# RMSNorm's weight before two gemms and its 1/rms behind them, in one decoder layer on one core

## The chip, the cores and the metric

One NeuronCore of a Trainium2 chip runs the whole program. The metric is device microseconds of one execution; the time of a kernel is the median of its runs. PE is TensorE, DVE is VectorE, ACT is ScalarE, POOL is GpSimd, and SP (SyncE) issues the DMAs. A line number such as L900 is a line of the kernel before; in the kernel after, lines behind the edits have other numbers.

## The reference

One layer, 512 positions (SEQ), width 1024 (D_MODEL), feed-forward width 4096, all fp32. The first half, retention and windowed attention merged by gates, is not touched by the change. Its second half is:

```python
def rmsnorm(x, g):
    y = x * rsqrt(mean(x * x, axis=-1) + EPS)
    return y * g
...
x = x + merged @ w_o
x = x + square(relu(rmsnorm(x, g_mlp) @ w_up)) @ w_down
x = x + sigmoid(rmsnorm(x, g_ple) @ w_ple_gate) * (p_i @ w_ple_proj)
```

For a row of x, 1/rms is one number r. Since relu(r a)^2 = r^2 relu(a)^2, and a gemm is linear in each row, r may be applied at the output: as r^2 where the MLP's product is added to x, as r inside the sigmoid.

## The kernel before

**Numbers and tiles.** x lies in four row tiles `xs[t]` of 128 x 1024 (t = 0 to 3). Every fp32 operand of a gemm is split in a high and a low half, and each product is three matmuls (`mm3`, L256 to L258): high x high, high x low, low x high. For the weights, ACT makes the high half (`whi`, L223) and the DVE the low one (`wlo`, L224), from a raw tile of 128 x 1024 that SP loads. There are six raw buffers and four of each half. The weights follow one plan; `units(n)` takes the next n tiles and first prepares `AHEAD` = 2 more. Some tiles of the down projection are sums or differences of two loads, which the DVE makes first (L202, L205).

**Order.** The kernel is plain Python that emits the instructions; a scheduler then orders each engine's queue and hands out the buffers. Work that should stand between matmuls is put into a list with `later(lag, ...)`. `tick()`, called from inside the gemms, emits what has become due; `force(key)` emits everything up to the entry named.

**The tail** (`tail`) is the stage of the change:

1. The W_o gemm, in two halves of 512 output columns, added into `xs` by the DVE. The second half's consumer `last` also starts `norm_T` of the tile, which gives h2.
2. `norm_T` (L381 on): two Squares on ACT with a sum per row (L388), the mean on the DVE (L390, L354), the power -1/2 on POOL (L355), two tensor_scalar y = x r (L394), and per half of 512 columns a `split_T`: four transposes on PE into one PSUM bank (`pt`, L365), four copies on ACT with the weight's column as scale (L373) and four scalar_tensor_tensor of 128 x 128 on the DVE for the low half (L374).
3. Four FFN phases f = 0 to 3. Each has an up gemm over 1024 of the 4096 features (192 matmuls of 512 columns), relu and square, sums of quarters of the result (`seven_left`), and the down projection `seven_gemm`: seven products in place of eight. Its units run in the order 4, 3, 5 (first unit), 4, 3, 5 (second unit), then 2, 2, 1, 1, 7, 7, 6, 6; a unit is 12 matmuls. The finished products are added to or subtracted from the 512-column quarters of x by the DVE (`acc`, L900), right behind the product that ends them.
4. In the last phase `ready` runs `norm_T` on each tile for h3: tiles 0 and 1 behind product 7, tiles 2 and 3 behind product 6.
5. The gate gemm (`w_ple_gate`) in two halves, sigmoid on ACT (L1001), times the embedding product, plus x (L1002, L1003), and out. Before a tile's matmuls `need` forces h3 of that tile.

Of the kernel before, what the change touches and what calls it, by code (L numbers as in the profile page):

```python
# [11 lines left out]
F32 = mybir.dt.float32  # L12
F32R = mybir.dt.float32r
AF = mybir.ActivationFunctionType
ALU = mybir.AluOpType
AX = mybir.AxisListType

P = 128
S = 512
D = 1024  # L20
NT = S // P
KD = D // P
# [6 lines left out]
EPS = 1e-6  # L29
# [3 lines left out]
GG = (2, 4)  # L33
# [42 lines left out]
class Block:  # L76
# [183 lines left out]
    def rows_gemm(self, act, nk, consume, perm=False, group=2, need=None, wave=None, halves=False):  # L260

        banks = [None] * NT
        nu = nk // 2
        if wave is not None:
            us = []

            def part(t, u):
                if u == 0:
                    banks[t] = self.gbank()
                wh, wl = us[u]  # L270
                for k in range(2):
                    kk = 2 * u + k
                    sh, sl = self.stat(act, kk, t, perm)
                    self.mm3(banks[t], sh, sl, wh[:, k], wl[:, k], kk == 0, kk == nk - 1)
                if u == nu - 1:
                    consume(t, banks[t])

            for m in range(NT):
                self.pinned = True
                if m >= 2:  # L280
                    wave(m)
                us += self.units(1)
                if m < NT - 1:
                    for t in range(m):
                        part(t, m)
                self.force(("h", m, 1))
                if m < NT - 1:
                    for u in range(m + 1):
                        part(m, u)
                self.pinned = False  # L290
            for t in range(NT - 1):
                part(t, NT - 1)
                part(NT - 1, t)
                self.ahead(t + 1)
            part(NT - 1, NT - 1)
            return
        for u0 in range(0, nu, group):
            us = self.units(min(group, nu - u0))
            for t in range(NT):
                if need is not None:  # L300
                    need(t)
                if u0 == 0:
                    banks[t] = self.gbank()
                cols = [slice(0, 512)] if not (halves and t == NT - 1) else [slice(0, 256), slice(256, 512)]
                for c in cols:
                    if c.start:
                        banks[t] = self.gbank()
                    for u, (wh, wl) in enumerate(us):
                        for k in range(2):
                            kk = 2 * (u0 + u) + k  # L310
                            sh, sl = self.stat(act, kk, t, perm)
                            self.mm3(banks[t][:, c], sh, sl, wh[:, k, c], wl[:, k, c], kk == 0, kk == nk - 1)
                        if u0 + u < nu - 1:
                            self.tick()
                    if u0 + len(us) == nu:
                        if len(cols) > 1:
                            consume(t, banks[t], c)
                        else:
                            consume(t, banks[t])
                        self.tick()  # L320
# [61 lines left out]
    def norm_T(self, x, t, goff, dst, key, lag):  # L382

        nc = self.nc
        ss = self.small(2, "ss")
        for h in range(2):
            j = self.tmp("j")
            self.pin(nc.scalar.activation(j, x[:, h * 512 : (h + 1) * 512], AF.Square, accum_out=ss[:, h : h + 1]))  # L388
        s1 = self.small(1, "s1")
        nc.vector.tensor_tensor(s1, ss[:, 0:1], ss[:, 1:2], op=ALU.add)  # L390
        r = self.rstd(s1, 1, D)
        for h in range(2):
            y = self.tmp("y")
            nc.vector.tensor_scalar(y, x[:, h * 512 : (h + 1) * 512], r, None, op0=ALU.mult)  # L394
            gain = None if goff is None else lambda k: self.gcol[:, goff + k : goff + k + 1]
            self.later(lag, lambda y=y, h=h: self.split_T([y], t, gain, 4 * h, dst), (key, t, h))

    def new_act(self, nbig, s):
        return ([self.big(s + "h") for _ in range(nbig)], [self.big(s + "l") for _ in range(nbig)])
# [474 lines left out]
        nc.scalar.activation(R(hi), src, AF.Copy)  # L874
        nc.vector.tensor_tensor(R(lo), src, hi, op=ALU.subtract)

    def seven_gemm(self, U, xs, ready):


        nc = self.nc  # L880
        LEFT = {1: 3, 2: 4, 3: 0, 4: 6, 5: 1, 6: 5, 7: 2}
        banks = {}

        def product(m, bank, u, first, last):
            (wh, wl), = self.units(1)
            for p in range(2):
                if first:
                    banks[bank, p] = self.gbank() if m in (3, 4) else self.bank("pb")
                ps = banks[bank, p]
                for k in range(2):  # L890
                    kk = 2 * u + k
                    c = slice(LEFT[m] * 256 + p * P, LEFT[m] * 256 + (p + 1) * P)
                    sh, sl = (R(U[i][kk].rearrange("p a b -> p (a b)")[:, c]) for i in range(2))
                    self.mm3(ps, sh, sl, wh[:, k], wl[:, k], first and k == 0, last and k == 1, m != bank)
                self.tick()

        X = lambda i, j, p: xs[2 * i + p][:, 512 * j : 512 * (j + 1)]

        def acc(x, v, op=ALU.add):
            nc.vector.tensor_tensor(x, x, v, op=op)  # L900

        for u in range(2):
            for m in (4, 3, 5):
                product(m, m, u, u == 0, u == 1)
        m4 = []
        for p in range(2):
            t = self.tmp("m4")
            nc.scalar.activation(t, banks[4, p], AF.Copy)
            m4.append(t)
            acc(X(0, 1, p), banks[3, p])  # L910
            acc(X(0, 1, p), banks[5, p], ALU.subtract)
        for u in range(2):
            product(2, 4, u, False, u == 1)
        for p in range(2):
            acc(X(1, 0, p), banks[4, p])
            acc(X(1, 1, p), banks[4, p], ALU.subtract)
        for u in range(2):
            product(1, 1, u, u == 0, u == 1)
        for p in range(2):
            acc(m4[p], banks[1, p])  # L920
            acc(X(0, 0, p), m4[p])
            acc(X(1, 1, p), m4[p])
        for u in range(2):
            product(7, 5, u, False, u == 1)
        for p in range(2):
            acc(X(0, 0, p), banks[5, p])
            if ready is not None:
                ready(p)
        for u in range(2):
            product(6, 3, u, False, u == 1)  # L930
        for p in range(2):
            acc(X(1, 1, p), banks[3, p])
            if ready is not None:
                ready(2 + p)


    def tail(self, mx):
        nc, a = self.nc, self.a
        xb = [self.big("x1") for _ in range(2)]
        xs = [xb[t // 2].rearrange("p (t c) n -> p t (c n)", t=2)[:, t % 2] for t in range(NT)]  # L940
# [3 lines left out]
        def add(half):  # L944
            def f(t, ps):
                v = xs[t][:, half * 512 : (half + 1) * 512]
                nc.vector.tensor_tensor(v, v, ps, op=ALU.add)
            return f

        self.rows_gemm(mx, KD, add(0))  # L950
        h2 = self.new_act(2, "h2")

        def last(t, ps):
            add(1)(t, ps)
            self.norm_T(xs[t], t, 16, h2, "h2", 5)

        self.rows_gemm(mx, KD, last, group=4)

        h3 = None
        for f in range(NF // 2):  # L960
            U = [[self.big("uh") for _ in range(4)], [self.big("ul") for _ in range(4)]]
# [28 lines left out]
            ready = None  # L990
            if f == NF // 2 - 1:
                h3 = self.new_act(2, "h3")
                ready = lambda t: self.norm_T(xs[t], t, 24, h3, "h3", 2 if t < 2 else 0)
            self.seven_gemm(U, xs, ready)

        out = self.a["out"][0]
        for half in range(2):
            def fin(t, ps, i=slice(0, 512)):
                s, o = self.tmp("fs"), self.tmp("fo")
                c = slice(half * 512 + i.start, half * 512 + i.stop)  # L1000
                nc.scalar.activation(s[:, i], ps[:, i], AF.Sigmoid)  # L1001
                nc.vector.tensor_tensor(o[:, i], s[:, i], pp[half][:, t, i], op=ALU.mult)  # L1002
                nc.vector.tensor_tensor(s[:, i], o[:, i], xs[t][:, c], op=ALU.add)  # L1003
                nc.sync.dma_start(out[t * P : (t + 1) * P, c], s[:, i])

            self.rows_gemm(h3, KD, fin, need=lambda t: self.force(("h3", t, 1)), group=GG[half], halves=half == 1)

    def make_plan(self):
        a, w = self.a, self.w_in
# [53 lines left out]
```

## Time and profile before

| | |
|---|---|
| median of 3 runs | 1037.51 us (1036.36 to 1038.64) |
| the profiled execution | 1038.66 us, span 1036.7 us |
| mean granted TensorE clock | 0.996 |
| the tail in the span, roughly | 640 to 1036.7 us |
| down projection of phase 0 ends | 738 us |
| down projection of phase 3 ends, gate gemm starts | 984.6 us |

The span goes from the first to the last instruction; the profiled execution is 1.96 us longer than it, which lies around it. A row of a timeline has start, duration, engine, line, operation, output <- inputs, shape and xcount, and in brackets an idle time before it and what ended it. A row of grouped instructions has the count, then busy time, then the mean in ns of one, then the idle time before them. A duration reaches past the start of the next instruction on the same engine, so that equal instructions in a row start closer together than they last.

### The profile page before, as it was taken

To read this page: it belongs to the slowest core of one execution; us is meant where nothing else is said; L and a number is where in the kernel's file an instruction comes from. 1 tells how busy PE (TensorE), PEld (TensorE's weight loads), DVE (VectorE), ACT (ScalarE), POOL (GpSimd) and SP (SyncE) were. 2 spreads that over 40 slices of the span, in tenths; PEclk is the share of its full clock that TensorE was granted. 3 is DMA by queue.
4 is the path that set the end of the run, shared out by engine and by line. 5 is a ranking of instruction groups with operands and counts; after the bars stand their busy time and mean duration, and the time that the engine had idled before them with its cause. 6 is when DMAs were issued, how large, how long until landed. Compare 5 with 4: busy or idle time off the path is not lost.

```text
span 1036.7 us, 12913 instructions
## 1 busy us (share of the span) xinstructions
PE 1014.2 (98%) x4810; PEld 848.4 (82%) x4810; DVE 676.6 (65%) x1017; ACT 480.4 (46%) x1012; POOL 137.8 (13%) x126
## 2 busy tenths in 40 slices
PE   8998989999999999999999999999999999999998
PEld 6776878988987788888888888988888888888877
DVE  5588766767686743545343344679769877867983
ACT  6534635465452442535342323665455355355461
POOL 0264043123025501000010000000000000000000
PEclk9999999999999999999999999999999999999999
DMA  9532312323321222222323422354753753845711
GB/s 330 180 116 69 99 42 63 101 62 102 102 69 54 82 82 81 82 82 68 96 89 115 162 85 78 103 183 161 233 175 124 241 166 120 265 160 184 243 63 59
DMA packets 84766, 128.81 MB, mean 124 GB/s; under 512 B 6576, under 2 KB 39392, under 8 KB 84704
## 3 DMA queue, kind: packets, MB, share of 16 engines
q1 hardware_dynamic: 84704, 128.00, 38.7%
q8 instruction: 37, 0.61, 0.2%
q14 instruction: 25, 0.20, 0.1%
HBM read 123.77 MB, written 4.21 MB: 123 GB/s over the span
## 4 chain that ended last, share of the span: by engine, by line
PE 81%; DVE 8%; issue 2%; POOL 2%; ACT 1%; DMA 0%; DVEq 0%; ACTq 0%; POOLq 0%
PE pg L256 23%; PE pg L258 23%; PE pg L257 23%; DVE ro L510 2%; PE pb L256 2%; PE pb L258 2%; PE pb L257 2%; DVE wlo L224 1%; PE ph L522 1%; DVE wlo L229 1%; PE pt L365 1%; POOL r L355 1%; PE po L638 1%; PE sc L615 1%; DVE ro L512 1%
## 5 line engine op out<-in xcount | busy, mean ns | idle before, releaser
L256 PE MATMUL pg<-whi,hh 128*128 128x512 f32 x480 | 201.7, 421 | 1.6 <-ACT zn L552 0.8
L257 PE MATMUL pg<-wlo,hh 128*128 128x512 f32 x480 | 189.7, 395 | 2.1 <-DVE wlo L229 2.1
L258 PE MATMUL pg<-whi,hl 128*128 128x512 f32 x480 | 189.5, 395 | 0.0
L223 ACT ACTIVATE whi<-raw 128x1024 fp32r<-128x1024 f32 (+1 forms) x120 | 123.6, 1043 | 131.9 <-PE pg L257 39.0
L224 DVE TENSOR_TENSOR wlo<-raw,whi 128x1024 fp32r<-128x1024 f32 (+1 forms) x120 | 146.2, 1230 | 36.8 <-ACT whi L223 35.7
L229 DVE SCALAR_TENSOR_TENSOR wlo<-raw,gcol,whi 128x512 fp32r<-128x512 f32 (+1 forms) x184 | 122.2, 704 | 64.1 <-ACT whi L228 63.9
L228 ACT ACTIVATE whi<-raw,gcol 128x512 fp32r<-128x512 f32 (+1 forms) x184 | 107.4, 639 | 86.3 <-PE pg L258 53.1
L355 POOL TENSOR_TENSOR r<-v,mhalf 128x1 f32<-128x1 f32 (+1 forms) x52 | 40.5, 778 | 653.0 <-DVE v L354 653.0
L257 PEld LDWEIGHTS pg<-wlo,hh 128*128 128x128 f32 x480 | 99.3, 207 | 18.2 <-DVE wlo L229 4.6
L258 PEld LDWEIGHTS pg<-whi,hl 128*128 128x128 f32 x480 | 98.6, 205 | 17.4 <-DVE hl L379 0.4
L256 PEld LDWEIGHTS pg<-whi,hh 128*128 128x128 f32 x480 | 98.9, 206 | 16.2 <-ACT whi L228 1.2
L256 PE MATMUL pg<-h2h,whi 128*128 128x512 f32 (+1 forms) x288 | 105.5, 367 | 0.0
L257 PE MATMUL pg<-h2l,whi 128*128 128x512 f32 (+1 forms) x288 | 105.3, 366 | 0.0
L258 PE MATMUL pg<-h2h,wlo 128*128 128x512 f32 (+1 forms) x288 | 105.2, 366 | 0.0
L258 PEld LDWEIGHTS pg<-h2h,wlo 128*128 128x128 f32 x288 | 54.3, 189 | 8.8
L257 PEld LDWEIGHTS pg<-h2l,whi 128*128 128x128 f32 x288 | 54.3, 189 | 8.6
L256 PEld LDWEIGHTS pg<-h2h,whi 128*128 128x128 f32 x288 | 54.2, 189 | 8.7
L256 PE MATMUL pg<-hh,whi 128*128 128x512 f32 x128 | 52.4, 410 | 0.0
L257 PE MATMUL pg<-wlo,uh 128*128 128x512 f32 x128 | 50.1, 391 | 0.0
L258 PE MATMUL pg<-hh,wlo 128*128 128x512 f32 x128 | 50.0, 391 | 0.0
L257 PE MATMUL pg<-hl,whi 128*128 128x512 f32 x128 | 49.9, 390 | 0.0
L258 PE MATMUL pg<-whi,ul 128*128 128x512 f32 x128 | 49.9, 390 | 0.0
(176 smaller groups left out, 1838.4 us busy)
## 6 DMA issues: line engine op xcount, KB each, us to landing
raw<-in_w_down SPq DMA_DIRECT2D x80, 512.0 KB, 3.4
raw<-in_w_in SPq DMA_DIRECT2D x76, 512.0 KB, 3.8
raw<-in_w_up SPq DMA_DIRECT2D x32, 512.0 KB, 4.6
raw<-in_w_ret_out SPq DMA_DIRECT2D x8, 512.0 KB, 3.4
raw<-in_w_o SPq DMA_DIRECT2D x8, 512.0 KB, 3.5
raw<-in_w_ple_gate SPq DMA_DIRECT2D x8, 512.0 KB, 4.8
x<-in_x SPq DMA_DIRECT2D x8, 256.0 KB, 6.1
pp_dram<-pp SPq DMA_DIRECT2D x8, 256.0 KB, 4.1
```

The source lines that it names most:

```text
L223: self.pin(nc.scalar.activation(R(hi[:, i]), raw[:, i], AF.Copy))
L224: nc.vector.tensor_tensor(R(lo[:, i]), raw[:, i], hi[:, i], op=ALU.subtract)
L228: self.pin(nc.scalar.activation(R(hi[:, i]), raw[:, i], AF.Copy, scale=g))
L229: nc.vector.scalar_tensor_tensor(R(lo[:, i]), raw[:, i], g, hi[:, i], op0=ALU.mult, op1=ALU.subtract)
L256: t.matmul(ps, sh, mh, start=first, stop=False, skip_group_check=more)
L257: t.matmul(ps, sh, ml, start=False, stop=False, skip_group_check=more)
L258: t.matmul(ps, sl, mh, start=False, stop=last, skip_group_check=more)
L355: self.nc.gpsimd.tensor_tensor(r, v, self.mhalf[:, :w], op=ALU.pow)
L365: nc.tensor.transpose(ps[:, k * P : (k + 1) * P], part[:, k * P : (k + 1) * P], self.ident)
L510: nc.vector.tensor_tensor(v4(t2)[:, :, o0 : o0 + 64], v4(zn)[:, :, i0 : i0 + 64], bc(Sn[:, o0 : o0 + 64], 64), op=ALU.mult)
L512: nc.vector.tensor_tensor(o, t1, t2, op=ALU.add)
L522: self.nc.tensor.transpose(ps[:, t * P : (t + 1) * P], rots[t][:, h * HD : (h + 1) * HD], self.ident)
```

## The change

For both norms the weight alone is applied before the gemm. Two `gain` rows per norm, 128 x 512, are loaded by DMA with the same row on every partition, into the buffers (`tabp`, four of them) that earlier tables held. `gain_T` is a tensor_tensor y = x gain of one half and a `split_T` without a scale, which splits the whole transposed half by one copy on ACT (L378) and one tensor_tensor on the DVE (L379). Since y does not wait for the row's mean, a half goes as soon as its 512 columns of x are final: h2's first halves behind the first half of W_o, h3's at each `done` in `seven_gemm`.

1/rms enters at the outputs. For the MLP, f2 holds 1/(mean + eps) and its negative, and every addition of a product into x becomes a scalar_tensor_tensor x = v f2 + x with f2's column as scalar; the addition into `m4` stays as it was. For the gate, r3 is the scale of the sigmoid; `need` asks only for the first half of a tile's h3 while the first two units run.

```diff
+    def gain_row(self, name):
+        out = []
+        for h in range(2):
+            g = self.a[name][0]
+            t = self.tabp.tile([P, 512], F32, tag="tab", name=self.nm("gr"))
+            self.nc.sync.dma_start(t, bass.AP(tensor=g.tensor, offset=g.offset + 512 * h, ap=[[0, P], [1, 512]]))
+            out.append(t)
+        return out
+
+    def gain_T(self, x, t, h, gain, dst, key, lag):
+        y = self.tmp("y")
+        self.nc.vector.tensor_tensor(y, x[:, h * 512 : (h + 1) * 512], gain[h], op=ALU.mult)
+        self.later(lag, lambda: self.split_T([y], t, None, 4 * h, dst), (key, t, h))
+
+    def mean_squares(self, x, v):
+        ...
@@ seven_gemm
-        def acc(x, v, op=ALU.add):
-            nc.vector.tensor_tensor(x, x, v, op=op)
+        def acc(i, j, p, v, sign=0):
+            t, x = 2 * i + p, X(i, j, p)
+            c = sign * NT + t
+            nc.vector.scalar_tensor_tensor(x, v, f[:, c : c + 1], x, op0=ALU.mult, op1=ALU.add)
+
+        def done(i, j, p):
+            if ready is not None:
+                ready(2 * i + p, j)
...
-            acc(X(0, 1, p), banks[5, p], ALU.subtract)
+            acc(0, 1, p, banks[5, p], 1)
+            done(0, 1, p)
...
-            acc(X(1, 0, p), banks[4, p])
-            acc(X(1, 1, p), banks[4, p], ALU.subtract)
+            acc(1, 0, p, banks[4, p])
+            done(1, 0, p)
+            acc(1, 1, p, banks[4, p], 1)
...
-            acc(m4[p], banks[1, p])
-            acc(X(0, 0, p), m4[p])
-            acc(X(1, 1, p), m4[p])
+            nc.vector.tensor_tensor(m4[p], m4[p], banks[1, p], op=ALU.add)
+            acc(0, 0, p, m4[p])
+            acc(1, 1, p, m4[p])
...
-            acc(X(0, 0, p), banks[5, p])
-            if ready is not None:
-                ready(p)
+            acc(0, 0, p, banks[5, p])
+            done(0, 0, p)
@@ tail
-        self.rows_gemm(mx, KD, add(0))
+        g2, g3 = self.gain_row("g_mlp"), self.gain_row("g_ple")
...
+        def first(t, ps):
+            add(0)(t, ps)
+            self.gain_T(xs[t], t, 0, g2, h2, "h2", 5)
 
         def last(t, ps):
             add(1)(t, ps)
-            self.norm_T(xs[t], t, 16, h2, "h2", 5)
+            self.gain_T(xs[t], t, 1, g2, h2, "h2", 3)
+            self.mean_squares(xs[t], v2[:, t : t + 1])
 
+        self.rows_gemm(mx, KD, first)
         self.rows_gemm(mx, KD, last, group=4)
+        nc.vector.reciprocal(f2[:, :NT], v2)
+        nc.vector.tensor_scalar(f2[:, NT:], f2[:, :NT], -1.0, None, op0=ALU.mult)
...
-                ready = lambda t: self.norm_T(xs[t], t, 24, h3, "h3", 2 if t < 2 else 0)
+                halves = [0] * NT
+                def ready(t, j):
+                    self.gain_T(xs[t], t, j, g3, h3, "h3", 2 if (t < 2 or j == 0) else 0)
+                    halves[t] += 1
+                    if halves[t] == 2:
+                        v = self.small(1, "v")
+                        self.mean_squares(xs[t], v)
+                        nc.gpsimd.tensor_tensor(r3[:, t : t + 1], v, self.mhalf[:, :1], op=ALU.pow)
...
-                nc.scalar.activation(s[:, i], ps[:, i], AF.Sigmoid)
+                nc.scalar.activation(s[:, i], ps[:, i], AF.Sigmoid, scale=r3[:, t : t + 1])
...
+            def need(t, u0):
+                self.force(("h3", t, 0 if u0 < 2 and half == 0 else 1))
```

The scheduler moves instructions on the DVE and PE with it; up to the W_o gemm the orders are the same. The pieces below are the engines' queues, in order; the number behind an underscore tells buffers of one name apart.

The DVE in the last phase, before, up to the first `wlo` of product 6 (`wlo1594_8114`; `pb` are the banks of product 1 and of products 5 and 7, `raw1591` is that product's first weight):

```order
L205 TENSOR_TENSOR raw1591_8108<-raw1591_8108,raw21592_8110 128x1024
L900 TENSOR_TENSOR m41575_8012<-m41575_8012,pb1585_8067 128x512
L900 TENSOR_TENSOR m41576_8016<-m41576_8016,pb1586_8074 128x512
L900 TENSOR_TENSOR x11065_5176<-x11065_5176,m41575_8012 128x512
L900 TENSOR_TENSOR x11066_5177<-x11066_5177,m41575_8012 128x512
L900 TENSOR_TENSOR x11065_5176<-x11065_5176,m41576_8016 128x512
L900 TENSOR_TENSOR x11066_5177<-x11066_5177,m41576_8016 128x512
L224 TENSOR_TENSOR wlo1594_8114<-raw1591_8108,whi1593_8113 128x1024
```

The same place after (the first `wlo` of product 6 is `wlo1598_8103`, and `raw1599` is the weight of its second unit):

```order
L953 TENSOR_TENSOR m41571_7965<-m41571_7965,pb1587_8042 128x512
L953 TENSOR_TENSOR m41573_7971<-m41573_7971,pb1588_8049 128x512
L927 SCALAR_TENSOR_TENSOR x11065_5176<-m41571_7965,f2_5195,x11065_5176 128x512
L379 TENSOR_TENSOR h3l1543_7843<-pt1589_8056,h3h1541_7841 128x4x128
L927 SCALAR_TENSOR_TENSOR x11066_5177<-m41571_7965,f2_5195,x11066_5177 128x512
L379 TENSOR_TENSOR h3l1543_7843<-pt1594_8078,h3h1541_7841 128x4x128
L927 SCALAR_TENSOR_TENSOR x11065_5176<-m41573_7971,f2_5195,x11065_5176 128x512
L927 SCALAR_TENSOR_TENSOR x11066_5177<-m41573_7971,f2_5195,x11066_5177 128x512
L205 TENSOR_TENSOR raw1595_8097<-raw1595_8097,raw21596_8099 128x1024
L205 TENSOR_TENSOR raw1599_8118<-raw1599_8118,raw21600_8120 128x1024
L927 SCALAR_TENSOR_TENSOR x11065_5176<-pb1560_7897,f2_5195,x11065_5176 128x512
L224 TENSOR_TENSOR wlo1598_8103<-raw1595_8097,whi1597_8102 128x1024
```

Low halves of h3, the second pre-addition and one addition of product 7 now stand before that `wlo`; further up, from the first addition of product 4 on, stand two more low halves and four y that stood behind it.

PE at the start of product 6 in the last phase, before (`pg` are its banks, `uh` and `ul` the split left operands):

```order
L258 MATMUL pb1565_7951<-whi1589_8086,ul1492_7569 128x512
L256 MATMUL pg1558_7921<-whi1593_8113,uh1485_7562 128x512
L257 MATMUL pg1558_7921<-wlo1594_8114,uh1485_7562 128x512
L258 MATMUL pg1558_7921<-whi1593_8113,ul1489_7566 128x512
L256 MATMUL pg1558_7921<-whi1593_8113,uh1486_7563 128x512
```

and after:

```order
L258 MATMUL pb1561_7904<-whi1592_8068,ul1487_7521 128x512
L256 MATMUL pg1554_7874<-whi1597_8102,uh1481_7515 128x512
L256 MATMUL pg1555_7881<-whi1597_8102,uh1481_7515 128x512
L257 MATMUL pg1554_7874<-wlo1598_8103,uh1481_7515 128x512
L258 MATMUL pg1554_7874<-whi1597_8102,ul1485_7519 128x512
L256 MATMUL pg1554_7874<-whi1597_8102,uh1482_7516 128x512
```

A second matmul that needs only the high half now stands ahead of the first that needs the low one. Four groups of transposes of h3, which stood behind this place, stand before it.

PE at the last unit of product 6 in phase 0, before (`whi1249` and `wlo1250` are the unit's weight):

```order
L258 MATMUL pg1211_6060<-whi1245_6245,ul1145_5572 128x512
L256 MATMUL pg1210_6053<-whi1249_6266,uh1142_5569 128x512
L257 MATMUL pg1210_6053<-wlo1250_6267,uh1142_5569 128x512
L258 MATMUL pg1210_6053<-whi1249_6266,ul1146_5573 128x512
L256 MATMUL pg1210_6053<-whi1249_6266,uh1143_5570 128x512
```

and after (`h2h` and `h2l` belong to the next phase's up gemm, with its own weight `whi1248`):

```order
L258 MATMUL pg1207_6013<-whi1241_6198,ul1143_5557 128x512
L256 MATMUL pg1206_6006<-whi1245_6219,uh1140_5554 128x512
L256 MATMUL pg1207_6013<-whi1245_6219,uh1140_5554 128x512
L256 MATMUL pg1261_6283<-h2h1071_5190,whi1248_6239 128x512
L257 MATMUL pg1261_6283<-h2l1073_5192,whi1248_6239 128x512
L256 MATMUL pg1262_6284<-h2h1071_5190,whi1248_6239 128x512
L257 MATMUL pg1206_6006<-wlo1246_6220,uh1140_5554 128x512
```

Five matmuls, three of them of the next gemm, now stand ahead of the first that needs this unit's low half, where one stood.

More of the change, by code (lines that the diff above doesn't have):

```diff
@@ L300, in rows_gemm @@
                 if need is not None:
-                    need(t)
+                    need(t, u0)
                 if u0 == 0:
@@ L396, in norm_T @@
             self.later(lag, lambda y=y, h=h: self.split_T([y], t, gain, 4 * h, dst), (key, t, h))
+    def gain_row(self, name):
[11 more added lines that the diff above has]
+    def mean_squares(self, x, v):
+        nc = self.nc
+        ss = self.small(2, "ss")
+        for h in range(2):
+            j = self.tmp("j")
+            nc.scalar.activation(j, x[:, h * 512 : (h + 1) * 512], AF.Square, accum_out=ss[:, h : h + 1])
+        s1 = self.small(1, "s1")
+        nc.vector.tensor_tensor(s1, ss[:, 0:1], ss[:, 1:2], op=ALU.add)
+        nc.vector.tensor_scalar(v, s1, 1.0 / D, EPS, op0=ALU.mult, op1=ALU.add)
     def new_act(self, nbig, s):
@@ L875, in seven_left, with seven_gemm @@
         nc.vector.tensor_tensor(R(lo), src, hi, op=ALU.subtract)
-    def seven_gemm(self, U, xs, ready):
+    def seven_gemm(self, U, xs, f, ready):
         nc = self.nc
@@ L909, in seven_gemm @@
             m4.append(t)
-            acc(X(0, 1, p), banks[3, p])
-            acc(X(0, 1, p), banks[5, p], ALU.subtract)
+            acc(0, 1, p, banks[3, p])
+            acc(0, 1, p, banks[5, p], 1)
+            done(0, 1, p)
         for u in range(2):
@@ L931, in seven_gemm @@
         for p in range(2):
-            acc(X(1, 1, p), banks[3, p])
-            if ready is not None:
-                ready(2 + p)
+            acc(1, 1, p, banks[3, p])
+            done(1, 1, p)
     def tail(self, mx):
@@ L948, in add @@
             return f
-        self.rows_gemm(mx, KD, add(0))
+        g2, g3 = self.gain_row("g_mlp"), self.gain_row("g_ple")
         h2 = self.new_act(2, "h2")
+        v2 = self.const.tile([P, NT], F32, name="v2")
+        f2 = self.const.tile([P, 2 * NT], F32, name="f2")
+        r3 = self.const.tile([P, NT], F32, name="r3")
+        def first(t, ps):
+            add(0)(t, ps)
+            self.gain_T(xs[t], t, 0, g2, h2, "h2", 5)
         def last(t, ps):
             add(1)(t, ps)
-            self.norm_T(xs[t], t, 16, h2, "h2", 5)
+            self.gain_T(xs[t], t, 1, g2, h2, "h2", 3)
+            self.mean_squares(xs[t], v2[:, t : t + 1])
+        self.rows_gemm(mx, KD, first)
         self.rows_gemm(mx, KD, last, group=4)
+        nc.vector.reciprocal(f2[:, :NT], v2)
+        nc.vector.tensor_scalar(f2[:, NT:], f2[:, :NT], -1.0, None, op0=ALU.mult)
         h3 = None
@@ L992, in tail @@
                 h3 = self.new_act(2, "h3")
-                ready = lambda t: self.norm_T(xs[t], t, 24, h3, "h3", 2 if t < 2 else 0)
-            self.seven_gemm(U, xs, ready)
+                halves = [0] * NT
[6 more added lines that the diff above has]
+                        nc.gpsimd.tensor_tensor(r3[:, t : t + 1], v, self.mhalf[:, :1], op=ALU.pow)
+            self.seven_gemm(U, xs, f2, ready)
         out = self.a["out"][0]
         for half in range(2):
+            def need(t, u0):
+                self.force(("h3", t, 0 if u0 < 2 and half == 0 else 1))
             def fin(t, ps, i=slice(0, 512)):
@@ L1004, in fin @@
                 nc.sync.dma_start(out[t * P : (t + 1) * P, c], s[:, i])
-            self.rows_gemm(h3, KD, fin, need=lambda t: self.force(("h3", t, 1)), group=GG[half], halves=half == 1)
+            self.rows_gemm(h3, KD, fin, need=need, group=GG[half], halves=half == 1)
     def make_plan(self):
```

## The prediction

> **What bounds the kernel now.** I read the head of the page, then the table of busy time by stage, then the waits and instructions of the last stage.
>
> ```profile
> span 1036.7 us, 12913 instructions
> PE 1014.2 (98%) x4810; PEld 848.4 (82%) x4810; DVE 676.6 (65%) x1017; ACT 480.4 (46%) x1012; POOL 137.8 (13%) x126
> ```
>
> The 65% of the DVE is a mean. The stages differ (columns: stretch, its length, then busy time and count of PE, PEld, DVE, ACT, POOL, granted clock, DMA share, GB/s):
>
> ```profile
> 640.00:670.00 30.00, 30.00 (x208) 27.62 (x208) 20.44 (x52) 17.07 (x47) 2.56 (x3) 1.00 0.29 89
> 720.00:738.00 18.00, 18.00 (x80) 14.73 (x79) 17.91 (x23) 7.16 (x8) 0.00 (x0) 1.00 0.79 246
> 960.00:975.00 15.00, 15.00 (x68) 12.44 (x67) 14.92 (x19) 4.13 (x4) 0.00 (x0) 1.00 0.77 249
> ```
>
> TensorE is never idle in these three, at full clock, and busy 98% of the whole span, so it is the bound: work taken off other engines gives nothing by itself. But at the end of a seven-product gemm (720 to 738 is the first, 960 to 975 the last) the DVE is busy 14.92 of 15 us. There PE is the bound only as long as the DVE brings the low halves of the weights (`wlo`) in time. How near that is, in the last stage:
>
> ```profile
> 972.15 0.39 PE L256 MATMUL pb<-whi,uh 128*128 128x512 f32 x1
> 977.59 0.39 PE L256 MATMUL pg<-whi,uh 128*128 128x512 f32 x1
> 977.82 0.39 PE L257 MATMUL pg<-wlo,uh 128*128 128x512 f32 x1
> 980.54 0.49 PE L257 MATMUL pg<-wlo,uh 128*128 128x512 f32 x1
> 982.03 0.66 PE L365 MATMUL pt<-ident,y 128*128 128x128 f32 x4 [0.30 <-DVE y L394]
> 1031.60 0.28 PE L256 MATMUL pg<-whi,h3h 128*128 128x256 f32 x1
> 1032.20 0.28 PE L258 MATMUL pg<-whi,h3l 128*128 128x256 f32 x1
> ```
>
> Matmuls of 512 columns start (977.59 − 972.15)/24 = 0.227 us apart, those of 256 columns 0.60/5 = 0.12. Product 6, first unit, takes its first `wlo` at 977.82, the second unit at 980.54; and the transposes wait once for y. On the DVE, from the first subtraction of product 4 out of x to those two `wlo` (start, busy):
>
> ```profile
> 959.19 1.28 DVE L900 TENSOR_TENSOR x<-x,pg 128x512 f32<-128x512 f32 x2
> ...
> 968.68 2.35 DVE L224 TENSOR_TENSOR wlo<-raw,whi 128x1024 fp32r<-128x1024 f32 x2
> ...
> 973.28 2.49 DVE L900 TENSOR_TENSOR x<-x,m 128x512 f32<-128x512 f32 x4
> 975.69 1.21 DVE L224 TENSOR_TENSOR wlo<-raw,whi 128x1024 fp32r<-128x1024 f32 x1
> ...
> 979.25 1.23 DVE L224 TENSOR_TENSOR wlo<-raw,whi 128x1024 fp32r<-128x1024 f32 x1
> ```
>
> The first unit's `wlo` ends at 976.90, 0.92 before PE takes it; the second's at 980.48, 0.06 before. That 0.92 is what the change has to spend.
>
> **The prices.** On the DVE what counts is the pitch, start to start in a row of equals:
>
> ```profile
> 263.95 2.73 DVE L229 SCALAR_TENSOR_TENSOR wlo<-raw,gcol,whi 128x512 fp32r<-128x512 f32 x4
> 87.01 0.74 DVE L229 SCALAR_TENSOR_TENSOR wlo<-raw,gcol,whi 128x512 fp32r<-128x512 f32 x1
> L900 DVE TENSOR_TENSOR x<-x,pg 128x512 f32<-128x512 f32 x32 | 20.4, 680 | 0.4 <-PE pg L258 0.4
> L806 DVE SCALAR_TENSOR_TENSOR At<-ry,r,G 128x256 f32<-128x256 f32 x16 | 7.7, 484 | 10.6 <-POOL r L355 10.6
> L867 DVE TENSOR_TENSOR z<-z 128x256 f32<-128x256 f32 x16 | 6.7, 420 | 20.4 <-ACT z L975 20.4
> L229 DVE SCALAR_TENSOR_TENSOR wlo<-raw,gcol,whi 128x512 fp32r<-128x512 f32 x120 | 93.7, 815 | 31.5 <-ACT whi L228 31.3
> L379 DVE TENSOR_TENSOR hl<-pt,hh 128x512 fp32r<-128x512 f32 x8 | 5.2, 683 | 4.3 <-ACT hh L378 4.3
> L1003 DVE TENSOR_TENSOR fs<-fo,x 128x512 f32<-128x512 f32 x7 | 4.8, 689 | 0.2
> L394 DVE TENSOR_SCALAR y<-x,r 128x512 f32<-128x512 f32 x24 | 10.7, 483 | 5.2 <-POOL r L355 5.0
> L374 DVE SCALAR_TENSOR_TENSOR h3l<-pt,gcol,h3h 128x128 fp32r<-128x128 f32 x32 | 9.6, 343 | 0.6 <-ACT h3h L373 0.5
> ```
>
> - Tensor_tensor of 512 columns: four in 2.49 us, one alone 0.68, so a pitch of (2.49 − 0.68)/3 = 0.60. The new y (x times gain) and the new low half of a transposed half are of this kind (689 and 683 ns alone): 0.60 each, where y was 0.40 (483 ns less the same 0.08 of overlap) and the low half four pieces of 0.26 (343 less 0.08).
> - Scalar_tensor_tensor with a column as scalar, the new addition into x: (2.73 − 0.74)/3 = 0.663, 0.063 more than now. On 256 columns the same step is 484 − 420 = 0.064. No row has it on 512 columns out of PSUM: the lower bound is nothing more (680 ns stays 680), the upper the mean of 815, that is 0.135 more. I take 0.063, because two pairs of rows agree on it.
> - `wlo` and the pre-additions (L205, L202), 1024 columns: 2.35 − 1.21 = 1.14.
>
> The Trainium skill, "VectorE: DVE Perf Modes", section "The DRAIN you can't avoid", speaks against the change: there the next vector operation does not start until the pipe has emptied. Taken so, each added operation would cost its full duration, some 0.08 more, and the ten or so added in the last stage 0.8 us more; four x in 2.49 us and not 2.72 say otherwise, so the pitch stands (by the page the time would be about 1041.1).
>
> **Before the FFN phases.** The gain rows add four DMAs on SP's queue. They take buffers that earlier tables held; SP stands behind each until the last reader is done, and what is queued behind it are weight loads. Three of the four stand where SP's next load is itself issued later than that reader's end. The other:
>
> ```profile
> 352.37 2.89 POOL L749 TENSOR_TENSOR qd<-hT,qdec 128x384 f32<-128x384 f32 x2 [2.89 <-DVE hT L145]
> 351.75 3.03 SPq L189 DMA_DIRECT2D raw<-in_w_in  x2
> ```
>
> It waits until 355.26, and the load behind it was issued about 354.4: 0.9 us late. Its cover is the loads' own lead, for raw buffers are six; without cover it costs 0.9. I take 0. In the W_o gemm the first halves' transposes move between the matmuls of the second half; there are still eight groups, on a PE that is busy 30.00 of 30, and DVE (20.44) and ACT (17.07) have room: 0. Leaving 1/rms out takes the POOL and two y out of the way of h2, but no PE wait stands there to be saved.
>
> **The first three phases.** Ahead of the last product's `wlo` stand 14 additions into x, now 0.063 longer: 0.88 us on a full DVE.
>
> ```profile
> 735.38 0.39 PE L256 MATMUL pg<-whi,uh 128*128 128x512 f32 x1
> 735.61 0.49 PE L257 MATMUL pg<-wlo,uh 128*128 128x512 f32 x1
> 734.32 3.50 DVE L224 TENSOR_TENSOR wlo<-raw,whi 128x1024 fp32r<-128x1024 f32 x3
> ```
>
> The first of the three is the last product's; it ends at 734.32 + 1.21 = 735.53, 0.08 ahead of PE. But in the new order PE has five matmuls, not one, before it: both high products of the unit and three of the next up gemm. So it is needed at 735.38 + 5 x 0.227 = 736.51 and is there at 736.41. I take 0.1 us for all three phases, for the next gemm's weight that is now wanted sooner; if the cover is gone, each loses 0.88 less its old slack, 0.8 in the first, at most 2.4 together.
>
> **The last phase, on the DVE.** From 959.19 to the same `wlo` of product 6, the new order has one addition into x more (13, not 12): 0.66; 12 of them 0.063 longer: 0.76; one more pre-addition, that of the second unit, which now stands before: 1.14; four y: 2.40; four low halves: 2.40. Together 7.4 us. The halves are made early, and so in front of the weights, where before every y and h3 stood behind them. ACT, which makes the high halves, is busy 4.13 of the 15 us and hides its one copy of 512 columns per half; POOL's 1/rms has the matmuls of a gate tile's gemm to be made before a sigmoid asks for it. The `wlo` ends at 976.90 + 7.4 = 984.3.
>
> **On PE.** Four groups of transposes now stand ahead of it. A group costs 0.35 and makes the next matmul 0.09 longer:
>
> ```profile
> 640.73 0.60 PE L365 MATMUL pt<-ident,y 128*128 128x128 f32 x4
> 641.08 0.48 PE L256 MATMUL pg<-whi,mh 128*128 128x512 f32 x1
> 641.39 0.40 PE L257 MATMUL pg<-wlo,mh 128*128 128x512 f32 x1
> ```
>
> That is 0.44 each, 1.76. With one more high product ahead (0.23), PE asks for the `wlo` at 977.82 + 1.76 + 0.23 = 979.8, or 980.2 where product 7's `wlo`, also behind early halves, has cost it some 0.4 (worked out in the same way). It then waits near 4 us: first for the high half, whose pre-addition ends about 981.3, then for the low one.
>
> From 984.3 on PE has left 190 matmuls of 512 columns (43.1), 48 of 256 (5.8) and four groups (1.7): 50.6 us, to 1034.9. Before, the last matmul ended at 1032.20 + 0.12 = 1032.3. The same count for before (191, 48, eight groups: 52.5) against the 54.5 us it took shows about 1.9 us of real losses there; I count them as gone. So +2.6. The sigmoid's column as scale adds 0.08 at the end, by:
>
> ```profile
> L829 ACT ACTIVATE gs<-pg,gcol 128x512 f32<-128x512 f32 x16 | 10.9, 681 | 23.1 <-PE pg L258 23.1
> L759 ACT ACTIVATE sg<-pg 128x512 f32<-128x512 f32 x8 | 4.8, 598 | 9.0 <-PE pg L258 8.9
> ```
>
> With 0.1 from the first phases the sum is +2.8 us. The profiled execution took 1038.66 us (span 1036.7, 1.96 around it), so it would take 1041.5; it lies 1.15 above the median of 1037.51, and against that the forecast is 1040.3.
>
> **The rivals.**
> 1. The early halves help. Over the whole end the DVE's work shrinks: 32 x 0.26 + 8 x 0.40 = 11.5 us go, 16 x 0.60 + 16 x 0.063 = 10.6 come, and the transposes are spread over a longer stretch, so the 1.9 us of losses behind product 6 vanish: 1037.5 − 1.9 = 1035.6. For it speaks the 0.30 wait for y; against it the full DVE from 960. It decides if the `wlo` of product 6 is ready by 980.2, 4.1 us before my sum: that is, if the early halves wait behind the weights on the DVE. The Trainium skill, "Perfetto Trace Analysis", section "Optimizing Scalar/DVE Operations", would side with it: grouping into larger operations raises throughput when the engine is saturated. The rows agree on the price (0.60 for four pieces of 0.26), but not on the place.
> 2. Half the stall. If the added operations are cheaper than bounded by their likes (additions at 680 ns: −0.8; y as cheap as the old, −0.8), the stall is 2.3 and the time 1038.7, within what counts as the same.
> 3. The first phases lose in full, 2.4 us in place of 0.1, and SP's late load its 0.9: 1042.6 with the first alone, 1043.5 with both. Against it stands the cushion of 0.9 per phase.
>
> **How the numbers follow.** Chances: forecast 0.58 (its own range 1039.0 to 1041.6), rival 1 0.12, rival 2 0.18, rival 3 0.12. A measurement of this kernel tells 0.2% from no change, 2.1 us: faster is below 1035.4, slower above 1039.6. Rival 1 gives 0.06 faster and 0.06 same; rival 2 0.17 same and 0.01 slower; of the forecast 0.08 falls into same. So 0.06, 0.31, 0.63. The range reaches from 1036.6, leaving out most of rival 1, to 1042.2, leaving out most of rival 3.
>
> **What would show it.** In the changed profile: PE waits of some 4 us in front of product 6's first unit, for `whi` and then `wlo`, and no other wait above 0.5 behind 950; the DVE without a gap from 960 to 985 with four y and four low halves before that `wlo`; the addition into x at about 740 ns; the end of the first three phases with waits under 0.3. I am wrong if the scalar form out of PSUM is as cheap as the plain one, if the DVE runs the weights ahead of the early halves, or if the phases before lose at each end.

## The result and the profile after

The changed kernel takes 1041.86 us (median of 5 runs, 1041.45 to 1044.69) against 1037.29 for the kernel before: the ratio is 1.0049 (95% interval 1.0035 to 1.0063). It is slower by 4.6 us, where 2.8 were forecast, and the forecast named the place. The profiled execution took 1041.72 us, 3.1 more than the one of before. But it starts the W_o gemm 2.2 us earlier than that one, though the orders up to there are the same (the last section comes back to that); from there on it loses 5.6 us.

The head of the page after:

```profile
span 1039.9 us, 12823 instructions
PE 1014.9 (98%) x4810; PEld 849.0 (82%) x4810; DVE 674.8 (65%) x971; ACT 471.5 (45%) x964; POOL 135.7 (13%) x122
```

All engines but PE have less to do, and PE has as many matmuls; the change did remove work. To see where the time went, the end of the program is cut in two: from the first matmul of W_o to the first of the last down projection, and from there to the start of the last matmul. Busy time by stretch, before and then after (stretch, length, busy time and count of PE, PEld, DVE, ACT, POOL, granted clock, DMA share, GB/s):

```profile
608.08:944.95 336.87, 336.87 (x1593) 283.04 (x1592) 243.79 (x304) 166.03 (x231) 4.39 (x5) 1.00 0.51 163
944.95:1032.20 87.25, 86.81 (x417) 71.34 (x415) 68.11 (x112) 41.94 (x80) 2.20 (x4) 1.00 0.42 143
```

```profile
605.86:943.01 337.15, 337.15 (x1594) 282.81 (x1592) 244.57 (x282) 160.95 (x207) 1.29 (x1) 1.00 0.50 162
943.01:1035.57 92.56, 89.03 (x417) 73.57 (x415) 66.72 (x88) 38.10 (x56) 3.11 (x4) 0.96 0.39 135
```

The first stretch grew by 0.28 us, the second by 5.31. In the second, PE is idle for 3.5 us, and the granted clock is 0.96. The waits of PE behind 640 us are two, and its instructions show them and what came behind:

```profile
PE pg L256 <- ACT whi L223: 2.6, 1, 2.6
PE pg L257 <- DVE wlo L224: 0.9, 1, 0.9
```

```profile
977.50 0.39 PE L258 MATMUL pb<-whi,ul 128*128 128x512 f32 x1
980.52 0.87 PE L256 MATMUL pg<-whi,uh 128*128 128x512 f32 x2 [2.63 <-ACT whi L223]
982.29 0.79 PE L257 MATMUL pg<-wlo,uh 128*128 128x512 f32 x1 [0.91 <-DVE wlo L224]
982.89 0.63 PE L258 MATMUL pg<-whi,ul 128*128 128x512 f32 x1
983.31 0.63 PE L256 MATMUL pg<-whi,uh 128*128 128x512 f32 x1
...
987.91 0.39 PE L257 MATMUL pg<-wlo,uh 128*128 128x512 f32 x1
988.14 0.40 PE L258 MATMUL pg<-whi,ul 128*128 128x512 f32 x1
```

This is product 6's first unit: first the high half is late, then the low one, together 3.54 us. These are idle times; from start to start the first gap is 980.52 − 977.50 = 3.02 us. With no wait PE would take the low half three matmuls behind 977.50, at 978.2; it takes it at 982.29, 4.1 us later. Behind it the matmuls start 0.43 us apart and not 0.227 until 987.9. Nothing waits there; the clock is down to about half, which is called half clock from here on:

```profile
980.00:983.00 3.00, 1.58 (x4) 0.91 (x5) 3.00 (x4) 2.92 (x4) 0.00 (x0) 0.66 0.73 234
983.00:988.00 5.00, 5.00 (x16) 3.98 (x15) 3.51 (x7) 2.75 (x7) 0.55 (x1) 0.52 0.88 303
```

The DVE ahead of that wait, from the changed timeline, and the price of the new addition:

```profile
956.96 1.40 DVE L927 SCALAR_TENSOR_TENSOR x<-pg,f,x 128x512 f32<-128x512 f32 x2
...
974.90 0.69 DVE L379 TENSOR_TENSOR h3l<-pt,h3h 128x512 fp32r<-128x512 f32 x1 [0.28 <-ACT h3h L378]
...
978.09 2.35 DVE L205 TENSOR_TENSOR raw<-raw,raw 128x1024 f32<-128x1024 f32 x2
...
981.02 2.35 DVE L224 TENSOR_TENSOR wlo<-raw,whi 128x1024 fp32r<-128x1024 f32 x2
```

```profile
L927 DVE SCALAR_TENSOR_TENSOR x<-pg,f,x 128x512 f32<-128x512 f32 x32 | 22.4, 743 | 0.2
```

The queue runs without a gap but for 0.28 us, and the low half ends at 981.02 + 1.21 = 982.2. It took 25.3 us from the addition at 956.96, where before the same queue took 17.7 (959.19 to 976.90).

### The profile page after: what moved, and what is told of

Same layout as the page of the kernel before. It is cut to its first block, busy times and chain, and to the rows that moved or that the text cites. A ratio compares the mean times of both kernels' runs of the same rounds, so it can differ in the third digit from the quotient of the medians.

```text
span 1039.9 us, 12823 instructions
## 1 busy us (share of the span) xinstructions
PE 1014.9 (98%) x4810; PEld 849.0 (82%) x4810; DVE 674.8 (65%) x971; ACT 471.5 (45%) x964; POOL 135.7 (13%) x122
## 4 chain that ended last, share of the span: by engine, by line
PE 85%; DVE 6%; POOL 1%; issue 1%; ACT 1%; DVEq 0%; ACTq 0%; POOLq 0%
PE pg L257 24%; PE pg L256 24%; PE pg L258 24%; PE pb L256 2%; PE pb L257 2%; PE pb L258 2%; DVE ro L535 2%; PE ph L547 1%; DVE wlo L229 1%; PE pt L365 1%; PE po L663 1%; POOL r L355 1%; PE sc L640 1%; DVE ro L537 1%; PE ry L825 1%
## 5 line engine op out<-in xcount | busy, mean ns | idle before, releaser
L355 POOL TENSOR_TENSOR r<-v,mhalf 128x4 f32<-128x4 f32 (+1 forms) x44 | 35.2, 799 | 271.1 <-DVE v L354 269.8
L1043 POOL TENSOR_TENSOR r<-v,mhalf 128x1 f32<-128x1 f32 x4 | 3.1, 776 | 386.7 <-DVE v L421 386.7
L256 PE MATMUL pg<-whi,uh 128*128 128x512 f32 x128 | 50.4, 398 | 2.6 <-ACT whi L223 2.6
```

The source lines that it names most:

```text
L256: t.matmul(ps, sh, mh, start=first, stop=False, skip_group_check=more)
L355: self.nc.gpsimd.tensor_tensor(r, v, self.mhalf[:, :w], op=ALU.pow)
```

## The experiments

Theory: all of the loss is product 6's wait, in two terms, its length and the half clock that the idle time sets off. Rivals: the longer additions cost it, or the clock fell for another reason.

**Late halves.** The two halves of a tile are started together, where the kernel before starts them:

```diff
             acc(0, 1, p, banks[5, p], 1)
-            done(0, 1, p)
...
             acc(1, 0, p, banks[4, p])
-            done(1, 0, p)
...
             acc(0, 0, p, banks[5, p])
             done(0, 0, p)
+            done(0, 1, p)
...
             acc(1, 1, p, banks[3, p])
+            done(1, 0, p)
             done(1, 1, p)
```

> The whole change, but each tile's two halves of h3 are started together, where the kernel before starts them (tiles 0 and 1 behind product 7, tiles 2 and 3 behind product 6). My theory: all of the +4.6 us comes from the early halves, as a PE stall of 3.5 us in front of product 6 and some 2.7 us of half clock behind it; without them the wlo of product 6 is in time, no matmul runs at half clock, and the 1.9 us of losses behind product 6 shrink: 1036.5 us, between 1035.5 and 1037.5. Rival A, the longer additions into x and the gain rows cost it: still 1039 or more. Rival B, half and half: about 1038.5.

Measured: 1035.45 us, ratio to before 0.9985 (0.9976 to 0.9995), 0.05 below the expected range. In this series and the three runs that follow, before took 1036.92. The same two stretches:

```profile
605.90:943.09 337.19, 337.19 (x1593) 282.76 (x1592) 244.58 (x282) 160.88 (x207) 1.28 (x1) 1.00 0.51 162
943.09:1028.96 85.87, 85.81 (x416) 71.72 (x415) 66.39 (x88) 37.59 (x56) 3.13 (x4) 1.00 0.43 145
```

The last stretch falls from 92.56 to 85.87 us, 1.4 below before, at full clock and with PE idle for 0.06 us. So with late halves the change gains there; the place of the halves cost it all.

**PE kept busy.** Twelve matmuls by a tile of zeros into product 6's banks:

```diff
+        if ready is not None:
+            for k in range(12):
+                nc.tensor.matmul(banks[3, k % 2], R(self.zero), wlast[0][:, 1], start=False, stop=False, skip_group_check=True)
         for u in range(2):
             product(6, 3, u, False, u == 1)
```

> The changed kernel, with twelve more matmuls by a tile of zeros, added into product 6's banks ahead of its first unit (the sums stay the same); ten of them stand where PE waits. The DVE's queue is untouched, so the stall's end is. My theory: the half clock behind the stall is set off by the idle time itself; with PE busy for 2.3 of the 3.0 us it does not come, and the time falls by 2.7 to about 1039.2 us, the matmuls behind the stall again 0.23 us apart. Rival, the clock falls for another reason (the load, the transfers at 303 GB/s there): half clock stays and the time is 1041.9 or above. Rival, added matmuls lengthen the path: up to 1044.

Measured: 1040.38 us, ratio 1.0034 (1.0022 to 1.0046). On PE, and the last stretch:

```profile
979.50 2.46 PE L965 MATMUL pg<-whi,zero 128*128 128x512 f32 x10
981.80 0.64 PE L256 MATMUL pg<-whi,uh 128*128 128x512 f32 x2
983.47 0.50 PE L257 MATMUL pg<-wlo,uh 128*128 128x512 f32 x1 [1.03 <-DVE wlo L224]
983.81 0.40 PE L258 MATMUL pg<-whi,ul 128*128 128x512 f32 x1
984.05 0.40 PE L256 MATMUL pg<-whi,uh 128*128 128x512 f32 x1
```

```profile
944.50:1034.23 89.73, 88.69 (x428) 73.94 (x427) 66.59 (x88) 38.02 (x56) 3.11 (x4) 1.00 0.41 139
```

The low half still comes late, but the matmuls behind it start 0.23 us apart, at full clock and with transfers as dense as in the changed kernel (305 GB/s from 984 to 989). So the half clock came from idling, not from the load. The stretch is 2.83 us shorter than after, about the price of the half clock: the two zero matmuls that stand outside the wait (0.45 us) and a low half taken 0.6 us less late (3.5 against 4.1) nearly cancel. The mean granted clock of the other runs agrees: 0.996 to 0.998 in the five with zeros, 0.993 to 0.995 in the five of the changed kernel. The median fell by 1.5 us and not by the 2.7 expected: the profiled execution with zeros, which is the median, reached W_o 1.5 us later than the one of after (607.32 against 605.86).

**Early y on POOL.**

```diff
-    def gain_T(self, x, t, h, gain, dst, key, lag):
+    def gain_T(self, x, t, h, gain, dst, key, lag, eng=None):
         y = self.tmp("y")
-        self.nc.vector.tensor_tensor(y, ...)
+        (eng or self.nc.vector).tensor_tensor(y, ...)
...
-                    self.gain_T(xs[t], t, j, g3, h3, "h3", 2 if (t < 2 or j == 0) else 0)
+                    self.gain_T(xs[t], t, j, g3, h3, "h3", 2 if (t < 2 or j == 0) else 0, nc.gpsimd if not halves[t] else None)
```

> The changed kernel, but the y of the first-finished half of each tile (x times gain, four of 128x512) is made by POOL and not by the DVE. My theory: the DVE's queue ahead of product 6's wlo is 4 x 0.60 = 2.4 us shorter, the stall falls from 3.5 to about 1.1 us, which is too short for the clock to fall: 1041.9 - 2.4 - 2.7 = 1036.8 us. Rival, POOL slows the DVE while it runs or its y are late: 1038.5 to 1041. If the half clock comes with short stalls too: 1039.5.

Measured: 1040.62 us, ratio 1.0033 (1.0022 to 1.0045): the rival was right. POOL and DVE:

```profile
961.12 4.30 POOL L410 TENSOR_TENSOR y<-x,gr 128x512 f32<-128x512 f32 x2 [351.10 <-DVE x L927]
...
970.89 1.30 POOL L410 TENSOR_TENSOR y<-x,gr 128x512 f32<-128x512 f32 x1 [0.56 <-DVE x L927]
```

```profile
962.62 1.66 DVE L202 TENSOR_TENSOR raw<-raw,raw 128x1024 f32<-128x1024 f32 x1
964.20 2.31 DVE L205 TENSOR_TENSOR raw<-raw,raw 128x1024 f32<-128x1024 f32 x1
971.40 3.01 DVE L224 TENSOR_TENSOR wlo<-raw,whi 128x1024 fp32r<-128x1024 f32 x2
```

Beside POOL, three of the DVE's rows grow: 1.66 and 2.31 us and not 1.21, the pair 3.01 and not 2.35. So 2.2 of the 2.4 us are lost again. Other rows beside POOL keep their length (the addition out of PSUM at 961.95 takes 0.74). The Trainium skill, "Perfetto Trace Analysis", section "Optimizing Scalar/DVE Operations", says that POOL and DVE share a read port, so that offloading from one to the other may not help; these rows agree. What this run is below after is mainly the half clock, which did not come:

```profile
944.89:1034.65 89.76, 86.66 (x416) 71.58 (x415) 66.44 (x84) 38.02 (x56) 10.01 (x8) 1.00 0.41 139
```

The stretch is 2.80 us shorter than after, 2.37 of it busy time of PE. PE is idle for 3.1 us here, nearly as long as after, but in pieces: the largest gaps are 1.03 to 1.44 us, start to start.

**The MLP's part alone.** h3 by `norm_T`, no scale in the sigmoid:

```diff
-                def ready(t, j):
-                    ...
+                ready = lambda t: self.norm_T(xs[t], t, 24, h3, "h3", 2 if t < 2 else 0)
```

> Only the MLP's part of the change: h2 by the gain rows, the additions into x by scalar_tensor_tensor in all four phases; h3 by the norm as in the kernel before, no scale in the sigmoid. My theory: the cushion of moved matmuls hides the 0.88 us per phase, so 1037.0 to 1038.0 us, the same as before. Rival, the longer additions cost in every phase: 4 x 0.8 more, 1040.5.

Measured: 1038.42 us, ratio 1.0015 (1.0006 to 1.0023): 0.4 us above the expected range.

```profile
605.15:942.29 337.14, 337.14 (x1593) 282.79 (x1592) 244.69 (x282) 160.97 (x207) 1.29 (x1) 1.00 0.51 162
942.29:1030.47 88.18, 87.60 (x417) 71.29 (x415) 69.03 (x112) 41.55 (x80) 3.12 (x4) 1.00 0.42 142
```

Three of the four phases cost nothing (337.14, and the 0.27 over before lies ahead of the first down projection, which starts 92.24 us behind W_o and not 91.94). The last costs 0.93, about the 0.88 that 14 longer additions add to the DVE. That it shows only there fits h3, which follows in the DVE's queue; no run tells that apart.

**The gate's part alone.** Early halves, plain additions:

```diff
-            nc.vector.scalar_tensor_tensor(x, v, f[:, c : c + 1], x, op0=ALU.mult, op1=ALU.add)
+            nc.vector.tensor_tensor(x, x, v, op=ALU.subtract if sign else ALU.add)
```

> Only the gate's part of the change: the early halves of h3 and the scale in the sigmoid as in the changed kernel; h2 by the norm and plain additions into x in all phases. The DVE's queue ahead of product 6's wlo is the changed kernel's but for 13 additions, each 0.063 us shorter: 0.8 less. My theory: a stall of 3.5 - 0.8 = 2.7 us remains, its longest single gap falls from 3.0 to some 2.2 us start to start, below the 2.35 at which half clock was first seen, so no half clock: 1.7 us above before, 1038.6. If the half clock comes all the same: 1041.3. Rival, the early halves are harmless without the longer additions: 1036.9 or less.

Measured: 1040.23 us (11 runs, 1039.11 to 1043.64), ratio 1.0030 (1.0019 to 1.0041), between the two cases. Before took 1037.25 in this series and the runs that follow. In the profiled execution:

```profile
977.12 0.39 PE L258 MATMUL pb<-whi,ul 128*128 128x512 f32 x1
979.43 0.73 PE L256 MATMUL pg<-whi,uh 128*128 128x512 f32 x2 [1.92 <-ACT whi L223]
981.15 0.50 PE L257 MATMUL pg<-wlo,uh 128*128 128x512 f32 x1 [0.99 <-DVE wlo L224]
981.84 0.63 PE L256 MATMUL pg<-whi,uh 128*128 128x512 f32 x1
```

```profile
980.00:990.00 10.00, 9.01 (x37) 7.14 (x37) 8.39 (x15) 7.84 (x15) 1.00 (x2) 0.83 0.75 257
```

The stall is 2.9 us, 0.6 shorter than after, as the shorter additions make it. A gap of 2.31 us start to start did bring half clock here, against my expectation, but for 10 x 0.17 / 0.5 = 3.4 us only. After, by the same sum over 980 to 990 (clock 0.66), it is 6.8.

**The gate's part, late.** As the run before, with the late halves of the first:

```diff
-            done(0, 1, p)
...
-            done(1, 0, p)
...
             done(0, 0, p)
+            done(0, 1, p)
...
+            done(1, 0, p)
             done(1, 1, p)
```

> The gate's part alone, with each tile's two halves of h3 started together behind products 7 and 6; h2 by the norm and plain additions. My theory: the gain of the run with late halves (0.15%, 1.5 us) is the gate's part alone, and the MLP's part costs some 0.3 us in the W_o stage: 1035.1 us with before at 1036.9. Rival, the gain is from the MLP's part: 1036.5 or more.

Measured: 1033.95 us (5 runs, 1033.83 to 1036.31), ratio 0.9962 (0.9948 to 0.9976), 1.1 us below the expected time. It beats both kernels.

```profile
605.91:942.77 336.86, 336.86 (x1594) 282.96 (x1592) 243.87 (x304) 166.11 (x231) 4.38 (x5) 1.00 0.51 163
942.77:1028.30 85.53, 85.53 (x416) 71.76 (x415) 65.60 (x88) 37.69 (x56) 3.11 (x4) 1.00 0.43 146
```

The last stretch is 1.72 below before, and PE is never idle in it. The medians differ by 3.3; the other 1.6 lie outside these two stretches, and no run tells what part of them is chance. By the prediction's pitches its work is 336 x 0.2267 + 48 x 0.12 + 8 x 0.44 = 85.5 us: nothing is left to gain in it without taking PE work away.

**A stall of chosen length.** The late halves of the first run, with four or eight additions of zeros to product 6's first weight, ahead of its high half:

```diff
                 self.nc.vector.tensor_tensor(raw, raw, g0, op=ALU.add)
+                if i == self.slow:
+                    for m in range(4):      # or 8
+                        self.nc.vector.tensor_tensor(raw[:, m % 2], raw[:, m % 2], self.zrow, op=ALU.add)
```

> The kernel with late halves, and four additions of a row of zeros (128x512, 0.60 us each) on the DVE in the chain of product 6's first weight, ahead of its high half. PE then waits for whi with a gap of some 2.2 us start to start, and for wlo with one of 1.4: about as long in all as in the changed kernel, 3.5 us, but in no piece as long as its 3.0. If the half clock hangs on the single gap: no half clock, the time is that of the late halves + 3.5 = 1039 us. If it hangs on the sum of the waits: 1041.8, with matmuls 0.43 us apart behind the stall.

> As the run before, with eight such additions: the first gap is some 4.6 us, the stall in all 5.9. If a single gap above 2.35 us sets off half clock: some 12 matmuls and more 0.43 us apart behind it, time of the late halves + 5.9 + 2.8 = 1044.1 us. If the stall costs only its length: 1041.3.

Four: 1041.83 us (10 runs, 1039.41 to 1043.85), ratio 1.0037 (1.0026 to 1.0047). Eight: 1044.15 us (4 runs), ratio 1.0058 (1.0044 to 1.0072). The profiled executions, four and then eight (hi and lo matmuls are L260 and L261 there):

```profile
976.22 0.39 PE L262 MATMUL pb<-whi,ul 128*128 128x512 f32 x1
978.85 0.73 PE L260 MATMUL pg<-whi,uh 128*128 128x512 f32 x2 [2.25 <-ACT whi L227]
980.61 0.50 PE L261 MATMUL pg<-wlo,uh 128*128 128x512 f32 x1 [1.02 <-DVE wlo L228]
980.95 0.39 PE L262 MATMUL pg<-whi,ul 128*128 128x512 f32 x1
981.17 0.40 PE L260 MATMUL pg<-whi,uh 128*128 128x512 f32 x1
```

```profile
943.81:1033.26 89.45, 86.18 (x416) 71.61 (x415) 68.92 (x92) 37.99 (x56) 3.50 (x4) 1.00 0.40 140
```

```profile
980.98 1.22 PE L260 MATMUL pg<-whi,uh 128*128 128x512 f32 x2 [4.50 <-ACT whi L227]
982.74 0.80 PE L261 MATMUL pg<-wlo,uh 128*128 128x512 f32 x1 [0.54 <-DVE wlo L228]
```

```profile
943.69:1038.15 94.46, 89.43 (x417) 73.94 (x415) 71.54 (x96) 38.21 (x56) 3.50 (x4) 0.95 0.39 132
```

With eight the stretch is 8.59 longer than with late halves alone, against 5.9 + 2.8 = 8.7 expected: a stall costs its length (the low half is taken 6.0 us late) and the half clock. With four it is 3.58 longer and the clock stays at 1.00, though the gap is 2.63 us start to start. But the median of its runs is 2.4 above that profiled execution, which was the fastest of the ten, and equals the 1041.8 that was expected with half clock. The mean granted clock of each run fits that: 0.993 to 0.995 in the six runs above 1041 us, 0.996 to 0.998 in the four below. Where in those six the clock fell is not shown, since only the fastest has a trace. The sum of the waits does not decide it (3.3 us here without, 2.9 in the gate's part alone with), and no fixed length of one gap does (2.63 without, 2.31 with).

## Why the prediction was wrong in size and right in place

- **The place and the stall held.** Forecast: `whi`, then `wlo` of product 6's first unit late, PE taking the `wlo` at 984.3 and not 980.2, 4.1 us late; measured 4.1 from start to start, 2.63 + 0.91 = 3.54 of it idle. The DVE's queue to that `wlo` grew by 7.6 us (25.3 against 17.7) where 7.4 were summed; a gap of 0.28 is in it. (The additions at 959.19, where the count begins, are those of product 3, not subtractions of product 4; the count of 12 and 13 holds.)
- **The prices held.** Addition 743 ns (about 740 forecast), y 0.68, low half 0.69 alone.
- **The failed step is the one on PE behind the stall:** "From 984.3 on PE has left ... 50.6 us". It counts every matmul of 512 columns at 0.227 us. Some run at 0.43. Counted on from the changed kernel's own 982.29, the same 50.6 us lead to 1032.9; its last matmul ends at 1035.57 + 0.12 = 1035.7, 2.8 us later, and the run with zeros took away 2.83. Without them the last stretch is 89.73 − 87.25 = 2.5 us longer, and 2.6 was forecast. So the stall's term was right, and a second term that hangs on it, the half clock, stood at nothing.
- **The trace of before could have told it.** Its clock drops behind two idle stretches of the first half, and I read only stages at clock 1.00:

```profile
140.00:160.00 20.00, 16.72 (x82) 14.00 (x82) 11.62 (x17) 6.81 (x18) 7.10 (x5) 0.91 0.18 53
330.00:350.00 20.00, 16.70 (x77) 13.14 (x77) 16.44 (x20) 6.71 (x10) 16.06 (x12) 0.91 0.10 27
```

- **The first three phases:** 0.1 us forecast, none measured. The cushion of five matmuls held. The 0.28 us lie in the W_o stage and the first up gemm (92.27 us from W_o to the first down projection, 91.94 before), where I had taken 0.
- **Product 7** was to wait some 0.4 us; no such wait stands in the trace.
- **The 1.9 us of losses behind product 6** did go: the count from 982.29 leaves no room for them in the changed kernel, with late halves 1.4 are gained, with the gate's part alone and late 1.7. That is the first rival's sum; its condition, that the early halves stand behind the weights, is what the late runs make true.

## What to carry to other kernels

Price a new PE stall with two numbers: its length, and the half clock that may follow. Here it followed some gaps between matmul starts of 2.1 us and more, and not others up to 2.6. Look in the trace for the nearest idle stretch of that kind, and at the granted clock behind it. Work that is cheaper can still be dear where it stands: on an engine that is full and feeds the bound one, start it behind what the bound engine needs next, however early its inputs are ready.

## What the runs showed of the hardware

- **Half clock comes in pieces of about 3.4 us.** Length, from the granted clock of the stretch: 20 x 0.09 / 0.5 = 3.6 (the two rows of before above, where the clock is rounded), 3.4 in the gate's part alone, 6.8 after. With eight additions, 976 to 990 at 0.63, it is 14 x 0.37 / 0.5 = 10.4: one piece, two, three.

```profile
976.00:990.00 14.00, 8.97 (x28) 6.39 (x27) 13.16 (x21) 7.82 (x14) 0.93 (x1) 0.63 0.48 149
```

  The Trainium skill, "TensorE: Matmul & The Clock Gate", section "Part 1: The HAM clock gate (the "warmup" mystery)", states a free-running window of some 3.4 us, and the low clock after an idle one. The pieces agree with the length, and gaps that sometimes count and sometimes don't agree with a window that runs free. But gaps of 2.3 us were enough here, less than the idle window stated, and one of 2.12 near 67 us in the gate's part, late (its clock was 0.50 from 70 to 72):

```profile
60.00:80.00 20.00, 18.15 (x81) 14.74 (x80) 16.80 (x21) 8.49 (x29) 13.45 (x10) 0.91 0.25 77
```

- **It makes part of the spread from run to run.** The same two idle stretches near 150 and 340 us brought half clock in before's profile at both places, after's at one, and in the one of the MLP's part alone at neither. They reached W_o at 608.08, 605.86 and 605.15 us. The order is not strict: late halves, also with neither, reached it at 605.90. The mean granted clock of the runs without a trace points the same way: of the 24 runs of before in the series of the late halves, the two at 1.000 took 1035.0 us, the nine at 0.998 have a median of 1036.6 and the eight at 0.996 one of 1038.4. One run at 0.949, with 1036.8, falls out of this order.
